# First layer's entry: output blocks 0 and 1 of the convolution's input product together, one half of the sequence at a time

## The chip, the cores and the metric

The kernel runs on one core of a Trainium2 chip. The metric is the device time of one execution in microseconds. The core's engines run side by side, each through a queue of its own in program order: TensorE (PE; its weight loads are listed as PEld), VectorE (DVE), ScalarE (ACT), GpSimd (POOL) and SyncE (SP, which here only issues loads from HBM). They wait for each other by semaphores.

## The reference, cut to what matters

A two-layer trunk on a sequence of 1024 rows with 1024 features, all in float32. The first layer starts with a conditioned norm, a product with a 1024x3072 matrix and a short gated convolution; the change is in that start alone. The rest (output product, MLP, a shared key/value side, attention, second MLP) follows unchanged.

```python
c_act = jax.nn.silu(c)
mod = c_act @ ada_w[l] + ada_b[l]                 # 1024 -> 6*1024; layer 0 here
sh_m, sc_m, g_m, sh_f, sc_f, g_f = jnp.split(mod, 6, axis=-1)
h = rmsnorm(x, norm_g[l, 0]) * (1 + sc_m) + sh_m  # modulate
bcx = h @ w_in                                    # 1024 x 3072
b_gate, c_gate, xh = jnp.split(bcx, 3, axis=-1)
u = c_gate * xh
conv = conv1d(u, w_conv, 3 taps, causal, per feature) + b_conv
y = (b_gate * conv) @ w_out
```

## The kernel before, in words

Every float32 product is made of three products of split operands: `hi` is the operand rounded to TensorE's reduced float32, `lo` what is left of it, and `mm` issues lo·hi, hi·lo, hi·hi into one accumulator. `split_w` makes the two parts, hi on ACT and lo on DVE.

The product `h @ w_in` has its output features in 8 blocks of 128 for each of the three parts g (b, c and x). Blocks 0 and 1 are computed directly in `conv_phase`; blocks 2 to 7 come after it in pairs with a scheme of seven products out of eight (`all_pairs`, `triple`), for which `conv_phase` leaves sums and differences of the halves of h (`sums`: t1 to t4). The first matmul of that pair phase needs the `uplo` part of its first weights, and its third group of twelve needs the split tile `s`.

h is made feature block by feature block (k = 0..7) and half by half (512 rows of the sequence each). Row tiles of x (`y` in the rows) are loaded, normed by `norm_x` (squares and root on ACT, scaling on DVE), turned by four transposes on TensorE (`turn`), then scaled and shifted while they leave PSUM: two ACT instructions (hi, and the full value) and one on DVE (lo), in `scaled`. Scale and shift of block k (`sh`) come from `ada(k)`, four loads of 256 KB (`aw`), a weighted sum over eight slices on DVE (eight instructions on `av`, the 8 values of silu(c) per partition as weights), two matmuls against a column of ones that add over the partitions, and two small DVE instructions (`ada_end`).

Before, the phase goes through k once for block m = 0, with half 0 ahead and half 1 two blocks of k behind (`LAG`), and then through k again for m = 1, both halves. The weights of w_in come in pieces of 128x384 (`w`): one per k and m. Four PSUM banks of `bank_ps` and two of `mm_ps` hold the accumulators of three g and two halves. `evict` reads them.

PE and SP stand in the written order in this phase (`pinned`). On DVE and ACT a scheduler sets the order when the program is built, also against the work behind the phase: the weighted sums of the next conditioning (`acc<-raw,csil,acc`) and the first splits of the pair phase (`uphi`, `uplo`, `s`) stand in DVE's and ACT's queues among the phase's own instructions.

Vectors (gains, biases, taps) are loaded as rows and turned by TensorE into columns, `vecs` and `bias`; the loads stand on ACT's queue.

Of the kernel before, what the change touches and what calls it, by code (L numbers as in the profile page):

```python
# [17 lines left out]
P = 128  # L18
# [30 lines left out]
def trunk_kernel(ctx: ExitStack, tc: tile.TileContext, x, c, ada_w, ada_b, norm_g, conv_in_w, conv_w,  # L49
# [5 lines left out]
    def nm(s):  # L55
        uid[0] += 1
        return f"{s}_{uid[0]}"
# [38 lines left out]
    def row_tile():  # L96
        return yp.tile([P, D], F32, tag="y", name=nm("y"), bufs=NT)
# [29 lines left out]
    vrows, brows = rows_[:, :P], rows_[:, P:2 * P]  # L127
    r = 0
    for src, n in ((norm_g.rearrange("l v (k p) -> (l v k) p", p=P), 64),
                   (conv_w[0].rearrange("w (k p) -> (w k) p", p=P), 24),  # L130
                   (conv_b.rearrange("o (k p) -> (o k) p", p=P), 8),
                   (kv_norm_g.rearrange("(k p) -> k p", p=P), 8),
                   (q_a_norm_g.rearrange("o (k p) -> (o k) p", p=P), 3),
                   (kv_a_norm_g.rearrange("(k p) -> k p", p=P), 2)):
        nc.scalar.dma_start(vrows[r:r + n, :], src)
        r += n
    nc.scalar.dma_start(brows[0:96, :], ada_b.rearrange("l (k p) -> (l k) p", p=P))
    nc.scalar.dma_start(brows[96:112, :], kv_ada_b.rearrange("(k p) -> k p", p=P))
# [722 lines left out]
    def conv_phase():  # L861
# [22 lines left out]
        nc.tensor.transpose(p_[:, :VEC_ROWS], vrows[:VEC_ROWS, :], ident[:VEC_ROWS, :VEC_ROWS])  # L884
        nc.vector.tensor_copy(vecs, p_[:, :VEC_ROWS])
        p_ = tp_ps()
        nc.tensor.transpose(p_[:, :BIAS_ROWS], brows[:BIAS_ROWS, :], ident[:BIAS_ROWS, :BIAS_ROWS])
        nc.vector.tensor_copy(bias, p_[:, :BIAS_ROWS])
        g1 = cp.tile([P, KD], F32, name="g1")
        b1 = cp.tile([P, KD], F32, name="b1")  # L890
        nc.vector.tensor_scalar(g1, gain(0, 0), RMS, None, op0=ALU.mult)
        nc.vector.scalar_tensor_tensor(b1, bias[:, 8:16], 1.0, g1, op0=ALU.add, op1=ALU.mult)
# [11 lines left out]
        def ada_end(k, raw):  # L904
            p_ = tp_ps()
            acc = st.tile([P, 2 * P], F32, tag="av", name=nm("av"), bufs=2)
            nc.vector.tensor_scalar(acc, raw[:, 0, :], csil[:, 0:1], None, op0=ALU.mult)
            for i in range(1, KD):
                nc.vector.scalar_tensor_tensor(acc, raw[:, i, :], csil[:, i:i + 1], acc, op0=ALU.mult, op1=ALU.add)  # L909
            for j in range(2):  # L910
# [22 lines left out]
        def weights(k, m):  # L933

            raw = ad.tile([P, D], F32, tag=("acc", "gmb")[k % 2], name=nm("w"), bufs=1)[:, :3 * P]
            ld(raw.rearrange("p (g m) -> p g m", g=3),
               conv_in_w[0][k * P:(k + 1) * P, :].rearrange("p (g c) -> p g c", g=3)[:, :, m * P:(m + 1) * P])
# [6 lines left out]
        def products(w, k, half, acc):  # L944
            for g in (1, 0, 2):
                mm(acc[g, half], [q[:, g * P:(g + 1) * P] for q in w], ops[("1", "2")[k // 4] + ("1", "2")[half]][k % 4],
                   k == 0, k == KD - 1)

        def evict(m, acc):
            b, c_, u, v = (row_tile() for _ in range(4))  # L950
            for half in range(2):
                sl = slice(half * HALF, (half + 1) * HALF)
                nc.scalar.activation(c_[:, sl], acc[1, half], AF.Copy)
                nc.scalar.activation(b[:, sl], acc[0, half], AF.Copy)
                nc.vector.tensor_tensor(u[:, sl], acc[2, half], c_[:, sl], op=ALU.mult)

            def end():
                conv(v, u, m, 0, S)
                nc.vector.tensor_tensor(v, v, b, op=ALU.mult)
                nc.scalar.dma_start(hd[m], v)  # L960

            late.append(end)

        def banks6():
            t_ = [bank_ps() for _ in range(4)] + [mm_ps(), mm_ps()]
            return {(g, half): t_.pop() for half in range(2) for g in (1, 0, 2)}

        def sums(kk):
            a, b = new[kk]
            c_, d = halves(row_tile())  # L970
# [15 lines left out]
        def first_half(k):  # L986
            raw = ada(k)
            if k == 0:
                load_x(0)
                norm_x(0)  # L990
            elif k == LAG:
                load_x(1)
            p_ = turn(k, 0)
            ada_end(k, raw)
            scaled(k, p_, old(k), ("11", "21")[k // 4])

        def second_half(k):
            if k < 4:
                new[k] = halves(raw_tile())
            scaled(k, turn(k, 1), new[k % 4][k // 4], ("12", "22")[k // 4])  # L1000

        with pinned([mybir.EngineType.PE, mybir.EngineType.SP]):
            w = [weights(0, 0)]
            first_half(0)
            acc = banks6()
            for k in range(KD + LAG):
                if k < KD - 1:
                    w.append(weights(k + 1, 0))
                    first_half(k + 1)
                if k < KD:  # L1010
                    products(w[k], k, 0, acc)
                if k == LAG:
                    norm_x(1)
                    second_half(0)
                if k >= LAG:
                    if k - LAG < KD - 1:
                        second_half(k - LAG + 1)
                    products(w[k - LAG], k - LAG, 1, acc)
                if k == KD:
                    w.append(weights(0, 1))  # L1020
            w = w[KD]
            st.release()
            evict(0, acc)
# [569 lines left out]
```

## Time and profile before

| | us |
|---|---|
| three runs, median (lowest, highest) | 2157.41 (2154.37, 2158.88) |
| profiled execution | 2159.2 |
| its span, first to last instruction | 2157.4 |
| PE busy in the span | 2062.0 (96%) |
| DVE busy, ACT busy | 1541.2 (71%), 1084.3 (50%) |
| first matmul of the pair phase starts at | 117.75 |

A matmul's busy time is modelled, so distances between starts say more than the busy time. An engine's idle time counts only where that engine carries the chain of work that ends last. The row of the granted clock has two levels for TensorE, 1.2 GHz (0.5) and 2.4 GHz (1.0).

### The profile page before, as it was taken

What the parts mean: (1) busy time and instruction counts of PE and PEld (TensorE: products, weight loads), DVE (VectorE), ACT (ScalarE), POOL (GpSimd) and SP (SyncE); (2) the same over time, 40 slices, a digit from 0 to 9 for tenths busy, and PEclk for the clock granted to TensorE, in tenths of its full rate; (3) what the DMA queues carried; (4) which work ended last, traced back from release to release, by engine and by line L of the source; (5) the groups of instructions that cost most, each with busy time, mean ns of one, the idle gap of its engine ahead of it and who ended that gap; (6) DMA issues with size and microseconds to landing.
All of it is one profiled execution on the core that took longest, in us unless ns stands there. A gap on an engine that the chain in (4) does not pass through costs nothing.

```text
span 2157.4 us, 25064 instructions
## 1 busy us (share of the span) xinstructions
PE 2062.0 (96%) x9438; PEld 1688.2 (78%) x9438; DVE 1541.2 (71%) x2087; ACT 1084.3 (50%) x1533; POOL 5.3 (0%) x13
## 2 busy tenths in 40 slices
PE   4999999989999999999899999999899999999998
PEld 3788878768888788888677788887678888788886
DVE  6877876876665669977688887756875665566576
ACT  4533353745554444455665565555744444544443
POOL 0000000000000000000000000000000000000000
PEclk9999999999999999999999999999999999999999
DMA  7444464254553889656223331143254653774355
GB/s 223 121 138 147 137 205 133 88 184 161 182 181 139 280 292 322 208 166 211 69 70 120 97 96 35 59 135 138 71 185 150 215 180 134 266 252 158 98 175 167
DMA packets 251023, 344.47 MB, mean 160 GB/s; under 512 B 19253, under 2 KB 142482, under 8 KB 250902
## 3 DMA queue, kind: packets, MB, share of 16 engines
q1 hardware_dynamic: 208408, 252.50, 37.4%
q10 hardware_dynamic: 42494, 90.38, 11.3%
q8 instruction: 74, 1.21, 0.2%
q14 instruction: 47, 0.39, 0.1%
HBM read 258.94 MB, written 83.89 MB: 159 GB/s over the span
## 4 chain that ended last, share of the span: by engine, by line
PE 77%; DVE 11%; ACT 6%; DMA 3%; issue 2%; ACTq 0%; SPq 0%; DVEq 0%
PE one L156 42%; PE mm L156 20%; PE tp L156 7%; PE big L156 3%; PE big L1360 2%; ACT junk L271 2%; DVE y L327 1%; PE tp L1386 1%; DVE raw L328 1%; DMA aw<-in_ada_w_dram 1%; ACT slot L1210 1%; DVE av L909 1%; PE tp L433 1%; DVE ring L160 1%; DVE acc L186 1%
## 5 line engine op out<-in xcount | busy, mean ns | idle before, releaser
L156 PE MATMUL one<-slot,uphi 128*128 128x512 f32 x1224 | 377.8, 389 | 0.0
L156 PEld LDWEIGHTS one<-slot,uphi 128*128 128x128 f32 x1224 | 230.4, 188 | 48.3 <-issue 0.5
L156 PE MATMUL one<-ring,ring 128*128 128x512 f32 x1152 | 262.9, 389 | 2.3 <-DVE ring L160 2.3
L160 DVE TENSOR_TENSOR uplo<-raw,uphi 128x1024 fp32r<-128x1024 f32 x127 | 153.3, 1222 | 143.1 <-ACT uphi L159 143.1
L156 PEld LDWEIGHTS one<-ring,ring 128*128 128x128 f32 x1152 | 215.9, 188 | 48.3 <-ACT ring L159 3.1
L156 PE MATMUL one<-slot,uplo 128*128 128x512 f32 x612 | 240.7, 393 | 8.2 <-DVE y L528 3.8
L160 DVE TENSOR_TENSOR ring<-raw,ring 128x1024 fp32r<-128x1024 f32 x144 | 174.3, 1220 | 55.6 <-ACT ring L159 55.3
L159 ACT ACTIVATE ring<-raw 128x1024 fp32r<-128x1024 f32 x144 | 149.5, 1052 | 106.6 <-DMA raw<-ha 61.6
L159 ACT ACTIVATE uphi<-raw 128x1024 fp32r<-128x1024 f32 x127 | 134.7, 1061 | 118.6 <-PE one L156 82.3
L156 PE MATMUL mm<-ring,ring 128*128 128x512 f32 x768 | 185.0, 390 | 1.6 <-DVE ring L160 1.6
L156 PE MATMUL tp<-ring,ring 128*128 128x512 f32 x768 | 183.9, 389 | 0.0
L159 ACT ACTIVATE ring<-w 128x1024 fp32r<-128x1024 f32 x80 | 84.8, 1060 | 178.7 <-PE tp L156 102.7
L156 PEld LDWEIGHTS mm<-ring,ring 128*128 128x128 f32 x768 | 143.7, 188 | 32.1 <-DVE ring L160 2.5
L156 PEld LDWEIGHTS tp<-ring,ring 128*128 128x128 f32 x768 | 144.1, 188 | 29.9
L160 DVE TENSOR_TENSOR ring<-w,ring 128x1024 fp32r<-128x1024 f32 x80 | 97.8, 1222 | 81.1 <-ACT ring L159 81.1
L156 PEld LDWEIGHTS one<-slot,uplo 128*128 128x128 f32 x612 | 115.2, 188 | 35.8 <-DVE y L528 5.5
L186 DVE SCALAR_TENSOR_TENSOR acc<-raw,csil,acc 128x1024 f32<-128x1024 f32 x88 | 112.5, 1278 | 22.8 <-DMA raw<-in_ada_w_dram 18.0
L526 ACT ACTIVATE y<-one 128x512 f32<-128x512 f32 x66 | 39.0, 591 | 159.6 <-PE one L156 118.5
L156 PE MATMUL mm<-slot,uphi 128*128 128x512 f32 x344 | 109.2, 399 | 9.6 <-DVE slot L398 9.4
L156 PE MATMUL one<-slot,s 128*128 128x512 f32 x468 | 112.9, 390 | 1.1 <-DVE s L160 1.1
L156 PEld LDWEIGHTS one<-slot,s 128*128 128x128 f32 x468 | 87.6, 188 | 20.6 <-DVE s L160 2.4
L156 PE MATMUL one<-q,uphi 128*128 128x512 f32 x328 | 101.9, 392 | 0.0
(267 smaller groups left out, 3614.4 us busy)
## 6 DMA issues: line engine op xcount, KB each, us to landing
ha<-y ACTq DMA_DIRECT2D x224, 256.0 KB, 4.0
raw<-ha SPq DMA_DIRECT2D x112, 512.0 KB, 4.0
raw<-in_ada_w_dram SPq DMA_DIRECT2D x80, 512.0 KB, 4.3
raw<-in_mlp_up_w_dram SPq DMA_DIRECT2D x70, 512.0 KB, 4.5
w<-in_mlp_down_w_dram SPq DMA_DIRECT2D x48, 512.0 KB, 7.0
raw<-in_mlp_down_w_dram SPq DMA_DIRECT2D x32, 512.0 KB, 4.0
raw<-in_conv_in_w_dram SPq DMA_DIRECT2D x18, 512.0 KB, 4.1
xs<-raw ACTq DMA_DIRECT2D x18, 512.0 KB, 2.8
```

Source lines behind the costliest of these rows:

```text
L156: nc.tensor.matmul(out_, lhs[a], rhs[b], start=first and i == 0, stop=last and i == 2, skip_group_check=more)
L159: nc.scalar.activation(hi, src, AF.Copy)
L160: nc.vector.tensor_tensor(lo, src, hi.bitcast(F32), op=ALU.subtract)
L186: nc.vector.scalar_tensor_tensor(acc, raw, s, acc, op0=ALU.mult, op1=ALU.add)
L271: nc.scalar.activation(junk, src, AF.Square, accum_out=ss)
L327: nc.vector.scalar_tensor_tensor(y, y, rroot(ss), self.gmb, op0=ALU.mult, op1=ALU.mult)
L328: nc.vector.tensor_tensor(xr, xr, y, op=ALU.add)
L433: nc.tensor.transpose(p_[:, t * P:(t + 1) * P], ys[half * 4 + t][:, k * P:(k + 1) * P], ident)
L526: nc.scalar.activation(dst, x_, AF.Copy)
L909: nc.vector.scalar_tensor_tensor(acc, raw[:, i, :], csil[:, i:i + 1], acc, op0=ALU.mult, op1=ALU.add)
L1210: nc.scalar.activation(y[32 * i:32 * i + 32, :], p_[32 * j:32 * j + 32, :], AF.Copy, scale=scale)
L1360: nc.tensor.matmul(o_, a, m_, start=j == 0, stop=j == 4)
```

## The change

Both output blocks m = 0 and 1 are computed together. A first pass over k does half 0 for both blocks, while scale and shift of block k arrive; a second pass does half 1 for both, from the weights' splits, all of which now stay (eight tiles each for hi and lo). A weight piece is 128x768 and holds both blocks: eight pieces instead of sixteen. Scale and shift of k = 0 and 1 are made by TensorE alone, sixteen matmuls of one column each with the loaded slices as weights, instead of the sum on DVE. x's first half is loaded first of all, its second half after all weights. Seven small row loads are cut into two groups: the gains of the norms and 96 rows of biases stay on ACT's queue, the others go to SP's, behind the loads of k = 0; the biases' transpose needs one of those. `sums` and the first stores take other buffers.

```diff
-    nc.scalar.dma_start(brows[96:112, :], kv_ada_b.rearrange("(k p) -> k p", p=P))
+    def later_rows():
+        ld(brows[96:112, :], kv_ada_b.rearrange("(k p) -> k p", p=P))
+        r = 0
...
+            ld(mrows[r:r + n, :], src)
+            r += n
...
-        def ada_end(k, raw):
-            p_ = tp_ps()
+        def ada_sum(raw):
             acc = st.tile([P, 2 * P], F32, tag="av", name=nm("av"), bufs=2)
...
+        def ada_end(k, raw, acc):
+            p_ = tp_ps()
             for j in range(2):
-                nc.tensor.matmul(p_[:, j:j + 1], acc[:, j * P:(j + 1) * P], ones[:, 0:1], start=True, stop=True)
+                cols = slice(j * P, (j + 1) * P)
+                if acc is not None:
+                    nc.tensor.matmul(p_[:, j:j + 1], acc[:, cols], ones[:, 0:1], start=True, stop=True)
+                else:
+                    for i in range(KD):
+                        nc.tensor.matmul(p_[:, j:j + 1], raw[:, i, cols], csil[:, i:i + 1], start=i == 0, stop=i == KD - 1)
...
-            w = [wr.tile([P, 3 * P], F32R, tag="w" + part_, name=nm("w"), bufs=4) for part_ in "hl"]
+            w = [wr.tile([P, 6 * P], F32R, tag="w" + part_, name=nm("w"), bufs=KD) for part_ in "hl"]
...
-        def products(w, k, half, acc):
+        def products(w, k, half, m, acc):
...
+            load_x(0)
+            raws, wraws, sums_, ws, turned = [], [], {}, [], {}
+
+            def fetch(k):
+                raws.append(ada(k))
+                wraws.append(weights(k))
+
+            fetch(0)
+            later_rows()
+            fetch(1)
+            feature_rows(vecs[:, :64], vrows[:64, :])
+            feature_rows(bias, brows[:BIAS_ROWS, :])
...
+            norm_x(0)
+
+            def scales(k):
+                ada_end(k, raws[k], sums_.get(k))
+                scaled(k, turned.pop(k), old(k), ("11", "21")[k // 4])
+                ws.append(weights_split(wraws[k]))
+
+            turned[0] = turn(0, 0)
+            scales(0)
+            turned[1] = turn(1, 0)
             acc = banks6()
-            for k in range(KD + LAG):
...
+            for k in range(KD):
+                if k + 2 < KD:
+                    fetch(k + 2)
+                    sums_[k + 2] = ada_sum(raws[k + 2])
+                elif k + 2 == KD:
+                    load_x(1)
+                    feature_rows(vecs[:, 64:VEC_ROWS], mrows[:VEC_ROWS - 64, :])
+                products(ws[k], k, 0, 0, acc)
+                if k + 1 < KD:
+                    scales(k + 1)
+                else:
+                    evict(0, 0, acc)
                     norm_x(1)
...
+                products(ws[k], k, 0, 1, acc)
+                if k + 2 < KD:
+                    turned[k + 2] = turn(k + 2, 0)
+            evict(1, 0, acc)
             st.release()
...
+            second_half(0, turn(0, 1))
+            second_half(1, turn(1, 1))
             acc = banks6()
             for k in range(KD):
-                w, w_ = weights(k + 1, 1) if k < KD - 1 else None, w
-                products(w_, k, 0, acc)
-                products(w_, k, 1, acc)
-                if k % 2 == 0:
-                    sums(k // 2)
-            evict(1, acc)
+                products(ws[k], k, 1, 0, acc)
+                if k + LAG < KD:
+                    second_half(k + LAG, turn(k + LAG, 1))
+                products(ws[k], k, 1, 1, acc)
+                if k + LAG >= 4 and k + LAG < KD:
+                    sums(k + LAG - 4)
+            for m in range(2):
+                evict(m, 1, acc)
```

PE's queue at the entry, before: the two transposes of the row vectors, then by k four transposes of x (`tp<-cs,y`) and the two matmuls against ones (`tp<-ones,av`), and the first products.

```order
L884 MATMUL tp_159<-cs,raw_82 128x109
L887 MATMUL tp_162<-cs,raw_82 128x112
L919 MATMUL tp_224<-cs,y_151 128x128
...
L911 MATMUL tp_229<-ones,av_230 128x1 x2
L919 MATMUL tp_263<-cs,y_151 128x128
...
L911 MATMUL tp_268<-ones,av_269 128x1 x2
L156 MATMUL mm_251<-slot_137,w_180 128x512
L156 MATMUL mm_251<-slot_137,w_179 128x512 x2
```

PE's queue at the entry, now (`tp<-csil,aw` is the conditioning by TensorE, sixteen matmuls for each of k = 0 and 1; w_255 is the lo part of the weights of k = 0, w_254 the hi part).

```order
L889 MATMUL tp_187<-cs,raw_82 128x64
L889 MATMUL tp_190<-cs,raw_82 128x112
L928 MATMUL tp_227<-cs,y_145 128x128
...
L920 MATMUL tp_232<-csil,aw_167 128x1 x16
L928 MATMUL tp_258<-cs,y_145 128x128
...
L158 MATMUL one_263<-slot_131,w_255 128x512
...
L920 MATMUL tp_294<-csil,aw_180 128x1 x16
L158 MATMUL one_266<-slot_131,w_255 128x512
```

The sixteen matmuls of k = 0 now stand between the first transposes and the first product, and those of k = 1 between the first product of block 0 and that of block 1.

DVE's queue in the first pass, now, from scale and shift of k = 1 on (w_317 is the lo part of the weights of k = 1, av_276 the weighted sum of k = 2, av_341 that of k = 3).

```order
L921 SCALAR_TENSOR_TENSOR sh_156<-tp_294,g_153,b_154 128x1
L923 TENSOR_TENSOR sh_156<-tp_294,bias 128x1
L935 TENSOR_TENSOR slot_131<-q_139,slot_131 128x512
L907 TENSOR_SCALAR av_276<-aw_269,csil 128x256
L162 TENSOR_TENSOR w_317<-w_185,w_316 128x768
L909 SCALAR_TENSOR_TENSOR av_276<-aw_269,csil,av_276 128x256 x5
L162 TENSOR_TENSOR w_368<-w_274,w_367 128x768
L909 SCALAR_TENSOR_TENSOR av_276<-aw_269,csil,av_276 128x256
L907 TENSOR_SCALAR av_341<-aw_334,csil 128x256
L909 SCALAR_TENSOR_TENSOR av_276<-aw_269,csil,av_276 128x256
```

The sum of k = 2 stands behind scale and shift of k = 1, so behind PE's sixteen matmuls for k = 1, and behind the split of the weights of k = 1.

DVE's queue at the end of the phase, before (uplo_1026, uplo_1059, s_201 and uplo_1069 are the pair phase's first splits; y_1007 is what the second block's last accumulators are read into).

```order
L160 TENSOR_TENSOR uplo_1026<-raw_1019,uphi_1025 128x1024
...
L160 TENSOR_TENSOR uplo_1059<-raw_1021,uphi_1058 128x1024
...
L160 TENSOR_TENSOR s_201_1064<-raw_1021,s_200_1063 128x512
L482 TENSOR_TENSOR raw_1019<-raw_1019,raw_1021 128x512
L186 SCALAR_TENSOR_TENSOR acc_1088<-raw_1096,csil,acc_1088 128x1024
L160 TENSOR_TENSOR uplo_1069<-raw_1019,uphi_1068 128x1024
L955 TENSOR_TENSOR y_1007<-one_756,y_1006 128x512
```

DVE's queue at the end of the phase, now (y_682 is read from the accumulator that PE finishes last, mm_715; uplo_987, uplo_1020 and s_172 are the same three splits).

```order
L970 TENSOR_TENSOR y_682<-mm_715,y_682 128x512
L188 SCALAR_TENSOR_TENSOR acc_1049<-raw_1052,csil,acc_1049 128x1024
L162 TENSOR_TENSOR uplo_987<-raw_980,uphi_986 128x1024
L188 SCALAR_TENSOR_TENSOR acc_1049<-raw_1054,csil,acc_1049 128x1024
L476 TENSOR_TENSOR raw_980<-raw_980,raw_982 128x512
L477 TENSOR_TENSOR raw_982<-raw_982 128x512
L188 SCALAR_TENSOR_TENSOR acc_1049<-raw_1057,csil,acc_1049 128x1024
L162 TENSOR_TENSOR uplo_1020<-raw_982,uphi_1019 128x1024
L481 TENSOR_TENSOR raw_982<-raw_982,raw_980 128x512
L484 TENSOR_TENSOR raw_980<-raw_980,raw_982 128x512
L162 TENSOR_TENSOR s_172_1025<-raw_982,s_171_1024 128x512
```

Before, the first splits stood ahead of the read of the last accumulator; now they stand behind it.

## Rows read from the trace of the kernel before

**Rows 1.** Windows: start:end, us, busy PE PEld DVE ACT POOL, clock, DMA share, GB/s.

```profile
0.00:117.53 117.53, 86.61 (x386) 69.47 (x386) 86.68 (x184) 60.76 (x103) 2.44 (x10) 0.97 0.62 179
117.53:200.00 82.47, 82.47 (x362) 67.60 (x361) 61.70 (x70) 27.81 (x35) 0.00 (x0) 1.00 0.40 124
```

**Rows 2.** Waits of PE, first 135 us: us in total, times, longest us.

```profile
PE tp L911 <- DVE av L909: 10.3, 4, 6.7
PE tp L884 <- DMA y<-in_x_dram: 9.6, 1, 9.6
...
PE tp L887 <- DMA raw<-in_kv_ada_b_dram: 2.7, 1, 2.7
```

**Rows 3.** Timeline of PE, end of the phase: start us, us, instruction, shapes, count.

```profile
115.03 2.88 PE L156 MATMUL one<-slot,w 128*128 128x512 f32 x12
117.75 0.39 PE L156 MATMUL one<-slot,uplo 128*128 128x512 f32 x1
123.19 1.07 PE L156 MATMUL one<-slot,s 128*128 128x512 f32 x4
```

**Rows 4.** Timeline of DVE, end of the phase; in brackets idle before and its releaser.

```profile
97.54 1.22 DVE L160 TENSOR_TENSOR uplo<-raw,uphi 128x1024 fp32r<-128x1024 f32 x1
...
110.21 0.68 DVE L160 TENSOR_TENSOR s<-raw,s 128x512 fp32r<-128x512 f32 x1
...
115.99 0.69 DVE L955 TENSOR_TENSOR y<-one,y 128x512 f32<-128x512 f32 x1 [2.13 <-PE one L156]
118.34 1.28 DVE L186 SCALAR_TENSOR_TENSOR acc<-raw,csil,acc 128x1024 f32<-128x1024 f32 x1 [1.67 <-DMA raw<-in_ada_w_dram]
```

**Rows 5.** Timeline of PE, 24 to 57 us.

```profile
24.46 0.98 PE L911 MATMUL tp<-ones,av 128*128 128x1 f32 x4 [1.89 <-DVE av L909]
25.31 2.91 PE L156 MATMUL mm<-slot,w 128*128 128x512 f32 x6
...
30.85 1.84 PE L156 MATMUL mm<-slot,w 128*128 128x512 f32 x6
...
55.68 0.60 PE L919 MATMUL tp<-cs,y 128*128 128x128 f32 x4
...
56.12 0.50 PE L911 MATMUL tp<-ones,av 128*128 128x1 f32 x4
56.48 1.63 PE L156 MATMUL mm<-slot,w 128*128 128x512 f32 x6
```

**Rows 6.** Windows of the loads and of the clock.

```profile
14.00:22.00 8.00, 3.09 (x11) 2.13 (x12) 6.61 (x18) 4.75 (x12) 0.00 (x0) 1.00 1.20 298
22.00:28.00 6.00, 4.11 (x13) 3.18 (x12) 5.12 (x14) 3.08 (x5) 0.00 (x0) 1.00 1.05 387
...
40.00:44.00 4.00, 3.50 (x10) 3.00 (x11) 3.12 (x9) 1.45 (x2) 0.00 (x0) 0.50 0.25 66
```

**Rows 7.** Timeline of ACT, norm of x's first and last tile of half 0.

```profile
10.55 1.06 ACT L271 ACTIVATE junk<-y 128x1024 bf16<-128x1024 f32 x1 [2.70 <-DMA y<-in_x_dram]
...
17.74 0.29 ACT L273 ACTIVATE small<-small,eps_d 128x1 f32<-128x1 f32 x1
```

**Rows 8.** Timeline of DVE, 41 to 45 us.

```profile
41.72 2.04 DVE L909 SCALAR_TENSOR_TENSOR av<-aw,csil,av 128x256 f32<-128x256 f32 x4
...
44.27 0.48 DVE L909 SCALAR_TENSOR_TENSOR av<-aw,csil,av 128x256 f32<-128x256 f32 x1
44.67 0.35 DVE L907 TENSOR_SCALAR av<-aw,csil 128x256 f32<-128x256 f32 x1
```

**Rows 9.** Groups by form, 0 to 117.5 us: count, busy us, mean ns, idle before.

```profile
L925 ACT ACTIVATE slot<-tp,sh 128x512 fp32r<-128x512 f32 x12 | 9.3, 778 | 21.7 <-DVE sh L914 19.0 <-DVE small L278 1.4 <-PE tp L919 1.3
...
L160 DVE TENSOR_TENSOR w<-w,w 128x384 fp32r<-128x384 f32 x16 | 8.8, 553 | 1.7 <-ACT w L159 1.7
...
L912 DVE SCALAR_TENSOR_TENSOR sh<-tp,g,b 128x1 f32<-128x1 f32 x8 | 1.7, 217 | 5.3 <-PE tp L911 5.3
```

**Rows 10.** Issues of loads, first 120 us: queue, count, KB, us to landing.

```profile
raw<-in_kv_ada_b_dram ACTq DMA_DIRECT2D x1, 8.0 KB, 5.6
```

More of the change, by code (lines that the diff above doesn't have):

```diff
@@ L126, in trunk_kernel @@
     rows_ = raw_tile()
[L127 to L136, printed above, removed]
[L137 to L138 removed]
+    vrows, brows, mrows = (rows_[:, i * P:(i + 1) * P] for i in range(3))
+    nc.scalar.dma_start(vrows[0:64, :], norm_g.rearrange("l v (k p) -> (l v k) p", p=P))
+    nc.scalar.dma_start(brows[0:96, :], ada_b.rearrange("l (k p) -> (l k) p", p=P))
+    def later_rows():
+        ld(brows[96:112, :], kv_ada_b.rearrange("(k p) -> k p", p=P))
+        r = 0
+        for src, n in ((conv_w[0].rearrange("w (k p) -> (w k) p", p=P), 24),
+                       (conv_b.rearrange("o (k p) -> (o k) p", p=P), 8),
+                       (kv_norm_g.rearrange("(k p) -> k p", p=P), 8),
+                       (q_a_norm_g.rearrange("o (k p) -> (o k) p", p=P), 3),
+                       (kv_a_norm_g.rearrange("(k p) -> k p", p=P), 2)):
+            ld(mrows[r:r + n, :], src)
+            r += n
     ones = cp.tile([P, P], F32, name="ones")
@@ L881, in load_x, with feature_rows @@
                 ld(xt[t], x0[t * P:(t + 1) * P, :])
-        p_ = tp_ps()
[L884 to L888, printed above, removed]
+        def feature_rows(dst, src):
+            p_ = tp_ps()
+            n = src.shape[0]
+            nc.tensor.transpose(p_[:, :n], src, ident[:n, :n])
+            nc.vector.tensor_copy(dst, p_[:, :n])
         g1 = cp.tile([P, KD], F32, name="g1")
         b1 = cp.tile([P, KD], F32, name="b1")
-        nc.vector.tensor_scalar(g1, gain(0, 0), RMS, None, op0=ALU.mult)
-        nc.vector.scalar_tensor_tensor(b1, bias[:, 8:16], 1.0, g1, op0=ALU.add, op1=ALU.mult)
         sh = [cp.tile([P, 2], F32, name=nm("sh")) for _ in range(KD)]
@@ L931, in conv_phase, with weights, weights_split @@
         new = [None] * 4
-        def weights(k, m):
-            raw = ad.tile([P, D], F32, tag=("acc", "gmb")[k % 2], name=nm("w"), bufs=1)[:, :3 * P]
+        def weights(k):
+            raw = ad.tile([P, D], F32, tag=("acc", "gmb")[k % 2], name=nm("w"), bufs=1)[:, :6 * P]
             ld(raw.rearrange("p (g m) -> p g m", g=3),
-               conv_in_w[0][k * P:(k + 1) * P, :].rearrange("p (g c) -> p g c", g=3)[:, :, m * P:(m + 1) * P])
-            w = [wr.tile([P, 3 * P], F32R, tag="w" + part_, name=nm("w"), bufs=4) for part_ in "hl"]
+               conv_in_w[0][k * P:(k + 1) * P, :].rearrange("p (g c) -> p g c", g=3)[:, :, :2 * P])
+            return raw
+        def weights_split(raw):
+            w = [wr.tile([P, 6 * P], F32R, tag="w" + part_, name=nm("w"), bufs=KD) for part_ in "hl"]
             split_w(w[0], w[1], raw)
@@ L942, in conv_phase, with evict @@
         late = []
-        def products(w, k, half, acc):
+        def products(w, k, half, m, acc):
             for g in (1, 0, 2):
-                mm(acc[g, half], [q[:, g * P:(g + 1) * P] for q in w], ops[("1", "2")[k // 4] + ("1", "2")[half]][k % 4],
+                mm(acc[m, g], [q[:, (2 * g + m) * P:(2 * g + m + 1) * P] for q in w], ops[("1", "2")[k // 4] + ("1", "2")[half]][k % 4],
                    k == 0, k == KD - 1)
[L949 to L955, printed above, removed]
+        kept_rows = [None, None]
+        def evict(m, half, acc):
+            if half == 0:
+                kept_rows[m] = [row_tile() for _ in range(2)]
+            b, u = kept_rows[m]
+            sl = slice(half * HALF, (half + 1) * HALF)
+            nc.scalar.activation(u[:, sl], acc[m, 1], AF.Copy)
+            nc.scalar.activation(b[:, sl], acc[m, 0], AF.Copy)
+            nc.vector.tensor_tensor(u[:, sl], acc[m, 2], u[:, sl], op=ALU.mult)
             def end():
+                v = row_tile()
                 conv(v, u, m, 0, S)
@@ L960, in end @@
                 nc.scalar.dma_start(hd[m], v)
-            late.append(end)
+            if half:
+                late.append(end)
         def banks6():
             t_ = [bank_ps() for _ in range(4)] + [mm_ps(), mm_ps()]
-            return {(g, half): t_.pop() for half in range(2) for g in (1, 0, 2)}
+            return {(m, g): t_.pop(0) for m in range(2) for g in (1, 0, 2)}
         def sums(kk):
             a, b = new[kk]
-            c_, d = halves(row_tile())
+            c_, d = halves(ad.tile([P, D], F32, tag=("acc", "gmb")[kk % 2], name=nm("w"), bufs=1))
             ops["t3"].append(block(kk))
@@ L984, in norm_x, with second_half @@
                 nc.vector.tensor_scalar(xt[t], xt[t], rroot(squares(nx, xt[t])), None, op0=ALU.mult)
[L986 to L997, printed above, removed]
+        def second_half(k, p_):
             if k < 4:
                 new[k] = halves(raw_tile())
-            scaled(k, turn(k, 1), new[k % 4][k // 4], ("12", "22")[k // 4])
+            scaled(k, p_, new[k % 4][k // 4], ("12", "22")[k // 4])
@@ L1021, in conv_phase @@
-            w = w[KD]
+            load_x(0)
[8 more added lines that the diff above has]
+            feature_rows(bias, brows[:BIAS_ROWS, :])
+            nc.vector.tensor_scalar(g1, gain(0, 0), RMS, None, op0=ALU.mult)
+            nc.vector.scalar_tensor_tensor(b1, bias[:, 8:16], 1.0, g1, op0=ALU.add, op1=ALU.mult)
```

19 lines of the change are left out of this document (2 added, 17 removed).

## Prediction

> **What bounds the kernel now.** I read the windows first, then PE's waits, then the timelines. The windows say where there is anything to win [rows 1]: in the entry phase PE is busy 86.6 of 117.5 us, behind it 82.5 of 82.5. From the pair phase on PE is the bound, without a gap, so the change is worth what it does to one moment: the start of the pair phase's first matmul, 117.75 us [rows 3]. The 30.9 us of PE's idle time in front of it are the whole stake. The waits split them [rows 2]: 9.6 us at the very start, until the first loads have landed, 2.7 more for the last bias row, and 10.3 us (one of 6.7) for DVE's weighted sums. The rest is pieces of one or two us. Then I looked at what stands ready when the phase ends [rows 4]: DVE made the first splits of the pair phase at 97.5 (`uplo`) and 110.2 (`s`), long before PE wants them at 117.75 and 123.19. The read of the last accumulators at 115.99 waits 2.13 us for PE and holds up nothing that PE needs.
>
> **The change, part by part.** PE's own work stays 288 matmuls of 512 columns and 64 transposes. At the upper rate twelve matmuls take 2.72 us (115.03 to 117.75) [rows 3], 0.227 each; four transposes 0.44 (55.68 to 56.12), the two matmuls of a conditioning block 0.36 (56.12 to 56.48) [rows 5]. At the lower rate the same are about 0.45 (2.91 for six, tail included) and 0.85 (24.46 to 25.31). The granted clock of 40 to 44 us is 0.50, which is 1.2 GHz [rows 6]; at PE's first start the rows say 1.00, but the spacing is that of the lower rate until about 31 us [rows 5, 6].
>
> *To the end of k = 0's conditioning (T0).* Before, the first x tile was normed from 10.55 on [rows 7], behind 0.2 MB of weights and 1.05 MB of slices; 1.77 MB at 298 GB/s [rows 6] are 5.9 us, so 4.6 us go to issue, first byte and completion. Now x comes first: at 387 GB/s, the rate of the stretch with x's other half [rows 6], its four tiles land at 6.0 to 10.0 us. From the first tile to the last root it took 7.5 us (10.55 to 18.03), with a weight split of 0.5 in it [rows 7]: 13.0, scaled at 13.9. The slices of k = 0 land at 13.5 (1.05 MB more at 298), the weights at 14.8, and behind those on the same queue the bias row that the biases' transpose waits for. PE takes its queue in order, so the transposes of x begin at about 15.3 and end at 16.2. Sixteen matmuls against two before: 8 x 0.85 = 6.8, T0 = 23.0.
>
> The bias row's landing, 5.6 us after its issue on ACT's queue [rows 10], was what PE waited for before, too [rows 2]. The Trainium skill (DMA: Bandwidth & Descriptors, "Queues, rings and completion order") says that each DMA engine takes turns between the queues that have work, packet by packet, so a small load on ACT's queue passes the large ones on SP's. The change takes that away. By that rule the row on its old queue would be there at about 12.7, as before, and T0 1.1 us earlier (x, at 13.9, then decides); by the queue order I use, 23.0. No run here shows the row on SP's queue.
>
> *To the end of k = 1's conditioning (T1).* Scale and shift, ACT's two instructions and DVE's lo: 0.4 + 1.5 [rows 9] + 0.7 (as the subtraction for `s`, [rows 4]), PE goes on at 25.65. Eight matmuls and the next sixteen: 1.8 + 2.9 at the upper rate, 3.6 + 6.8 at the lower, so T1 lies between 30.4 and 36.1. Sixteen one-column matmuls in a row don't occur before, so it is open whether they bring the clock up; before, the spacing fell 6.5 us after PE had begun to work through (24.46 to about 31) [rows 5]. I take T1 = 32: counted from T0, the same 6.5 us end at 29.5, when the eight matmuls (25.65 + 3.6) are through, and the sixteen run at the upper rate.
>
> *From T1 to k = 2.* DVE's queue decides, walked row by row as it now stands: scale and shift, ACT's scaling and the lo part end at T1 + 2.6. Then comes one step of the sum of k = 2, and then the split of the weights of k = 1, whose ACT half had to wait for the scaling of k = 1. A 768 wide split lies between 0.55 (384, [rows 9]) and 1.22 (1024, [rows 4]); I take 0.9. Five steps of the sum: 0.5 apart in a chain, 0.4 where another instruction stands between [rows 8]. With the split of k = 2's weights and the last steps the sum is ready at T1 + 8.1, PE has its scale and shift at T1 + 8.5. PE's work in that time is 4.5 us; it waits 4.
>
> *k = 3 to 7.* DVE per k: first step 0.3, seven steps 3.1 [rows 8], split 0.9, lo 0.6, scale and shift 0.2: 5.1. PE per k: 18 x 0.227 + 0.44 + 0.36 = 4.9. They are level, so each k costs the larger, plus what the lo part loses by standing among the sums, about 0.5: 5.6, five times 28. Then 2.05 (block 1 of k = 6), 0.5, and 3.9 for k = 7: half 0 ends at T1 + 43.1. Bounds: 4.9 per k if DVE never holds PE (3.5 us less), 6.6 if its interleaving costs a whole us more (5 us more).
>
> *Half 1.* Two groups of transposes, scaling, lo: PE waits 2.9 us at the change of halves, with x's second half long there. Sixteen groups of nine matmuls, 32.5, and six groups of transposes, 2.6: the phase ends at T1 + 81. DVE has 40 instructions of 0.6 to 0.7 there, 27 us, and keeps up. So the phase's matmuls end at 113, against 117.5: 4.5 us won.
>
> *The pair phase's start.* Here something is lost. The first splits now stand behind the read of the accumulator that PE finishes last. After PE's last matmul come that read (0.69), a step of a conditioning sum (1.28) and the split `uplo` (1.22) [rows 4]: 3.2 us in which PE has nothing. PE then has 24 matmuls, 5.4 us, to 8.6; `s` is ready only after another step (1.28), two sums of 0.6, a third step whose row must still land (about 6.4 + 1.2), a split of 1.15 (the same spacing as its 1.22 busy, less the overlap), two more of 0.6 and ACT's and DVE's parts of `s`: 10.8. Another 2.15. Together 5.35, between 0 and 8.
>
> The Trainium skill (TensorE: Matmul & The Clock Gate, "Architectural detail") says that VectorE's queue is strictly first in, first out, and that only TensorE pulls anything forward. By it the whole 5.35 is paid; if DVE could begin `uplo` while the read waits, nothing. The trace has no counterexample: behind the read at 115.99 nothing started during its wait of 2.13 [rows 4].
>
> *Sum.* 113.1 + 5.35 = 118.5 for the first gapless stretch, against 117.6: 0.9 us longer. The rest of the kernel is unchanged and PE-bound. The profiled execution took 2159.2, so 2160; the median of the runs shown is 1.8 below it, so 2158.3 there. I have counted no wait that I can't name, and add 0.7: 2159.
>
> **Rivals.** *Lower rate until T1 (slower).* Place: the two times sixteen matmuls. For it: at the start of before, the spacing fell only with full-width matmuls under way [rows 5]. Against it: PE is occupied without a gap from 16 us on. Price: T1 = 36, 4 us more, in all 5 more than before: 2163. It decides if the first products still have the 0.45 spacing at 29 us. Chance 0.18.
>
> *Loads late (slower).* The slices of k = 4 stand on SP's queue behind the weights of k = 3, and these wait for the split of k = 1 at T1 + 3.7. 1.44 MB at 298 GB/s and 3 us of latency put them at T1 + 11.5, and DVE wants the first half at T1 + 12.1. If each load comes 2 us later than that, DVE waits about 1.4 us in each of five k: 7 us, 2165. For it: PE's longest wait, 6.7 us for a sum [rows 2], came in the stretch with the densest loads. Against it: the second and later k have 2 us and more in hand. It decides from a wait of DVE for `aw` of over 1 us a k. Chance 0.15.
>
> *PE bound from k = 2 on (faster).* T1 = 30.4 and 4.9 per k: 1.6 + 3.5 less, 4.2 below before: 2153.5; without the wait at the pair phase 2148. For it: sums of two k are interleaved, which saves the chain's 0.1 per step. Against it: DVE's 5.1 is an even match at best. Chance 0.17.
>
> *Forecast:* no change that can be told, 0.5. About 0.2%, 4.3 us, is what a measurement of this kernel can tell from no change.
>
> **How the numbers follow.** The forecast's own range is T1 from 30.4 to 34 and the lower end of the waits, 2155 to 2162. To hold 8 in 10 it goes up over both slower rivals, to 2167, and down to half of the faster one with part of the pair phase's wait gone, 2149. Slower by over 0.2%: the two slower rivals nearly whole, less what of them stays within, 0.3. Faster: the faster rival and a little of the forecast's lower side, 0.2. Within: 0.5.
>
> **What would show it.** T0 near 23 and T1 near 32 in PE's timeline; the first pair matmul near 118 behind a gap of 3 us, and a second gap of 2 us before `s`; PE's wait for DVE `uplo` and `s` in its list of waits. If no such gaps are there, the term of 5.35 is wrong and the result is faster; if DVE waits for `aw`, the loads rival holds; if the spacing of the first products is 0.45, the clock rival.

## The result, and the profile after

The changed kernel takes 2167.02 us (median of 4 runs, 2163.4 to 2168.67) against 2156.96 for the one before (4 runs): ratio 1.0037, 95% interval 1.002 to 1.0054. The medians lie 10 us apart (0.47%), by the ratio of the runs it is slower by 0.37%, where 2159 and no change that can be told were forecast. The profiled execution took 2163.4 us, the lowest of the four; its span is 2161.5, 4.1 above that of before.

The windows of the changed kernel, cut where PE's last matmul of the phase ends, in the columns of [rows 1]:

```profile
0.00:116.15 116.15, 95.77 (x443) 78.10 (x443) 68.43 (x149) 55.89 (x91) 2.44 (x10) 0.97 0.52 151
116.15:200.00 83.85, 79.38 (x339) 64.45 (x339) 69.53 (x79) 29.16 (x36) 0.00 (x0) 0.98 0.51 156
```

Against [rows 1], PE idles 20 us in the phase where it idled 31, but its busy time rose by 9, and the stretch behind, gapless before, now has 4.5 us of idle time. DVE's work in the phase fell by 18 us (86.7 to 68.4). From PE's waits, first 135 us:

```profile
PE tp L917 <- DVE av L909: 0.9, 1, 0.9
```

The waits for DVE's sums [rows 2] fell from 10.3 to 0.9 us, as the change has it; a wait of 3.97 us for `uplo`, which before lay ready 19 us early [rows 4], is new. PE's timeline, to be read against [rows 3, 5]:

```profile
14.85 0.42 PE L889 MATMUL tp<-cs,raw 112*128 112x112 f32 x1 [10.74 <-DMA raw<-in_kv_ada_b_dram]
...
16.63 6.99 PE L920 MATMUL tp<-csil,aw 128*128 128x1 f32 x32 [0.51 <-DVE bias L890]
...
26.26 3.40 PE L158 MATMUL one<-slot,w 128*128 128x512 f32 x8 [0.60 <-DVE slot L935]
29.50 4.07 PE L920 MATMUL tp<-csil,aw 128*128 128x1 f32 x32
...
41.84 0.58 PE L917 MATMUL tp<-ones,av 128*128 128x1 f32 x4 [0.85 <-DVE av L909]
...
77.72 1.03 PE L928 MATMUL tp<-cs,y 128*128 128x128 f32 x8
...
114.63 1.52 PE L158 MATMUL mm<-slot,w 128*128 128x512 f32 x6
120.12 0.50 PE L158 MATMUL one<-slot,uplo 128*128 128x512 f32 x1 [3.97 <-DVE uplo L162]
...
128.00 3.06 PE L158 MATMUL one<-slot,s 128*128 128x512 f32 x12 [0.50 <-DVE s L162]
```

The sixteen one-column matmuls of a block show as 32 instructions. T0 is 16.63 + 6.99 = 23.6, T1 is 33.57, the phase ends at 116.15, and `s` is used at 128.00 against 123.19 [rows 3]: 4.8 us later. Matching PE's matmuls one by one against before, the distance is 4.2 to 5.0 nearly everywhere from there to the end (2.5 and 5.9 at the extremes), so the span's 4.1 us are the entry's.

### The profile page after: what moved, and what is told of

It is laid out like the page before. It is cut to its first block, busy times and chain, and to the rows that moved or that the text cites. A ratio compares the mean times of both kernels' runs of the same rounds, so it can differ in the third digit from the quotient of the medians.

```text
span 2161.5 us, 25112 instructions
## 1 busy us (share of the span) xinstructions
PE 2073.2 (96%) x9495; PEld 1698.2 (79%) x9495; DVE 1534.0 (71%) x2064; ACT 1082.2 (50%) x1525; POOL 5.3 (0%) x13
## 4 chain that ended last, share of the span: by engine, by line
PE 78%; DVE 12%; ACT 7%; DMA 2%; issue 2%; ACTq 0%; SPq 0%; DVEq 0%
PE one L158 42%; PE mm L158 20%; PE tp L158 7%; PE big L158 3%; PE big L1392 2%; ACT junk L273 2%; DVE y L329 1%; PE tp L1418 1%; DVE raw L330 1%; ACT slot L1242 1%; DVE acc L188 1%; DMA raw<-hd 1%; PE tp L435 1%; DVE ring L162 1%; PE tp L920 1%
```

## The experiments

Each was timed in five rounds against the kernel before, on one chip per group. T1 (end of block 1's conditioning on PE) and the start of the first `s` matmul are read from each profile's timeline of PE.

| kernel | conditioned by TensorE | T1 | `s` at | median us | ratio, 95% interval |
|---|---|---|---|---|---|
| before | none | 25.4 | 123.2 | 2157.2 to 2157.7 | |
| change, again | 0, 1 | 36.6 | 131.2 | 2167.53 | 1.0044, 1.0032 to 1.0056 |
| new order, sums on DVE | none | 26.0 | 118.4 | 2153.36 | 0.9982, 0.9974 to 0.9991 |
| new order, block 1 only | 1 | 30.7 | 124.1 | 2159.44 | 1.0007, 0.9998 to 1.0016 |
| old order | 0, 1 | 35.0 | 132.3 | 2171.41 | 1.0064, 1.0051 to 1.0078 |

The theory after the result: the one-column matmuls, at TensorE's lower rate, put more on the path than the sums they replace. The rivals: the order, and the new wait at the pair phase's start.

**The change again** (no edit).

> The changed kernel itself once more, for its size beside the others. Its profiled execution ended 4.1 us above the one of before, the median of its four runs 10.1 us. If the entry phase is all of the loss, the first pair-phase matmul and the total move together, and a profile with a total near 2167 shows a later end of the phase (a later rise of PE's rate, T1 2 to 5 us later) or a longer stretch at the lower rate behind the gap at the pair phase's start. If the loss is elsewhere, the phase ends near 116 again and the difference of 4 to 6 us appears behind 200 us. Ratio to before between 1.002 and 1.0054.

2167.53 us in 6 runs. The profiled execution took 2170.72, and its timeline of PE differs from the first one's where it counts:

```profile
26.25 3.78 PE L158 MATMUL one<-slot,w 128*128 128x512 f32 x8 [0.60 <-DVE slot L935]
29.82 6.82 PE L920 MATMUL tp<-csil,aw 128*128 128x1 f32 x32
...
123.21 0.50 PE L158 MATMUL one<-slot,uplo 128*128 128x512 f32 x1 [3.97 <-DVE uplo L162]
...
126.14 0.63 PE L158 MATMUL one<-slot,uplo 128*128 128x512 f32 x1
126.57 1.05 PE L158 MATMUL one<-slot,uphi 128*128 128x512 f32 x2
...
131.20 3.03 PE L158 MATMUL one<-slot,s 128*128 128x512 f32 x12 [0.66 <-DVE s L162]
```

Block 1's 32 instructions take 6.82 us, as block 0's do, not 4.07: T1 is 36.6, 3.1 later, and `s` 3.2 later. So the first profile had caught an execution in which the higher rate came early. What its span has beyond that comes at the very end, where nothing was changed: from the entry to 2100 us this execution stands 6 to 9 us behind before, and 4 more from 2128 us of before on. There PE waits 1.98 us for one of DVE's splits (0.65 before), and the thirty matmuls behind the next wait run in part at the lower rate. Before, then the repeat:

```profile
2130.61 7.11 PE L156 MATMUL mm<-ring,ring 128*128 128x512 f32 x30 [0.98 <-DVE ring L160]
```
```profile
2139.62 9.72 PE L158 MATMUL mm<-ring,ring 128*128 128x512 f32 x30 [0.90 <-DVE ring L162]
```

From 2140 to 2145 us of the repeat the granted clock is 0.50, at the same place before 1.00: 1.3 and 2.6 us make up the 4. No such end stands in the first profile, so these are of the execution and not of the change.

**Only the order: both sums back on DVE.**

```diff
+            for k in range(2):
+                sums_[k] = ada_sum(raws[k])
             turned[0] = turn(0, 0)
             scales(0)
```

> Undoes one part: scale and shift of blocks 0 and 1 by DVE's sums again, everything else as changed. Theory A (the sixteen matmuls stand on the path, nearly all at the lower rate, while DVE sits idle from 17 to 34 us): T0 falls from 23.6 to 17 to 19, T1 from 33.6 to 24 to 26, the phase ends 7 to 9 us earlier, total 7 to 9 us below the changed kernel. Rival B (the loads are the bound of the first pass, so an earlier T1 is given back by waits for slices): T1 is earlier, DVE waits for slices by 1 us or more per block, and the total moves by less than 3 us.

2153.36 us in 11 runs: 14 below the change, nearly twice what was expected, and 0.18% faster than before, its interval clear of 1. PE and, below, DVE:

```profile
16.65 1.01 PE L917 MATMUL tp<-ones,av 128*128 128x1 f32 x4 [0.75 <-DVE av L909]
...
25.05 0.98 PE L917 MATMUL tp<-ones,av 128*128 128x1 f32 x4 [0.96 <-DVE av L909]
...
118.37 3.04 PE L158 MATMUL one<-slot,s 128*128 128x512 f32 x12 [0.42 <-DVE s L162]
```
```profile
12.01 0.35 DVE L907 TENSOR_SCALAR av<-aw,csil 128x256 f32<-128x256 f32 x1
...
13.98 2.04 DVE L909 SCALAR_TENSOR_TENSOR av<-aw,csil,av 128x256 f32<-128x256 f32 x4
```

DVE makes block 0's sum from 12.0 on, while PE still waits for the bias row, so block 0 is conditioned at 17.7 instead of 23.6, block 1 at 26.0 instead of 36.6. The sums were not in the way here; DVE had the time. `s` comes 12.8 us earlier than in the repeat of the change.

**Block 0 on DVE, block 1 by TensorE** (`sums_[0]` alone).

> The change with block 0's sum on VectorE and block 1's alone by TensorE. Measured: both on VectorE 2153.4, both by TensorE 2167.5, 14.1 between them. Theory A, each block costs its own 32 small matmuls on the path at the lower rate: block 0 is ready at 17.7 as with both on VectorE, the products follow at 20.3, the 32 small ones take 6.8 from 24, so block 1's conditioning ends near 31 instead of 25.6: 2158.7 (2157 to 2161). Theory B, most of the cost is block 0's, which holds up the first product while all else waits, and block 1's is hidden behind VectorE's sum of block 2: 2155 or less. Theory C, the cost comes from both together through TensorE's rate: below 2157 or above 2162.

2159.44 us, at theory A's 2158.7. PE's timeline:

```profile
23.82 6.83 PE L920 MATMUL tp<-csil,aw 128*128 128x1 f32 x32
```

T1 is 30.7 (31 was expected). Block 1 by TensorE costs 6.1 us, block 0 the other 8.1, around the 6.8 us of a block's one-column matmuls; T1 moves by 4.6 and 6.0, the start of `s` by 5.7 and 7.1. So neither block's share is hidden behind other work.

**The other part alone: TensorE conditions blocks 0 and 1 in the old order.**

```diff
         def ada_end(k, raw):
             p_ = tp_ps()
...
+            if k > 1:
...
             for j in range(2):
...
+                cols = slice(j * P, (j + 1) * P)
+                if k > 1:
+                    nc.tensor.matmul(p_[:, j:j + 1], acc[:, cols], ones[:, 0:1], start=True, stop=True)
+                else:
+                    for i in range(KD):
+                        nc.tensor.matmul(p_[:, j:j + 1], raw[:, i, cols], csil[:, i:i + 1], start=i == 0, stop=i == KD - 1)
```

> The kernel before, in its own order, with one part of the change: the conditioning of blocks 0 and 1 by TensorE, 16 matmuls a block, in place of VectorE's sums. Its block 1's conditioning ends at 25.4 today. Theory A, the old order has room for it: block 1's conditioning ends about 5 to 6 later, but TensorE's wait of 6.67 us for VectorE's sum of block 3 shrinks by as much, since VectorE has 16 operations less to do: 2155 to 2159, no measurable difference. Theory B, the small matmuls are paid in full as in the new order: 6 to 14 slower, 2163 to 2171.

2171.41 us, 14.0 above before; I had expected theory A. The wait of 6.67 us that should have shrunk [rows 2] is still there, 9.7 us later. PE, then DVE:

```profile
19.22 6.83 PE L917 MATMUL tp<-csil,aw 128*128 128x1 f32 x32
...
27.96 6.99 PE L917 MATMUL tp<-csil,aw 128*128 128x1 f32 x32 [0.42 <-ACT q L931]
...
50.19 0.99 PE L914 MATMUL tp<-ones,av 128*128 128x1 f32 x4 [6.88 <-DVE av L910]
```
```profile
26.75 0.35 DVE L908 TENSOR_SCALAR av<-aw,csil 128x256 f32<-128x256 f32 x1
27.95 0.69 DVE L932 TENSOR_TENSOR slot<-q,slot 128x512 fp32r<-128x512 f32 x1 [0.85 <-ACT q L931]
34.99 0.22 DVE L918 SCALAR_TENSOR_TENSOR sh<-tp,g,b 128x1 f32<-128x1 f32 x1 [6.35 <-PE tp L917]
...
35.19 2.04 DVE L910 SCALAR_TENSOR_TENSOR av<-aw,csil,av 128x256 f32<-128x256 f32 x4
```

DVE has begun the sum of block 2 at 26.75 and then stands 6.35 us in front of block 1's scale, which PE delivers; the sum's other steps are queued behind it. So the work taken off DVE became a wait of DVE. With this the two parts add up: the order -3.8, TensorE's conditioning +14.0, together +10.2; the change measures +10.1 to +10.4. This profile is only some 9 us behind before all along. The other 5 us are a matter of which executions were profiled: this one, 2168.33, lies 3.1 below the median of its runs, and before's, 2159.2, lies 1.8 above that of its own.

**TensorE kept busy before its start.** To see what the lower rate is worth, 18 matmuls of the identity ahead of the bias rows' transpose (their result is not used).

```diff
+            p_ = tp_ps()
+            for i in range(18):
+                nc.tensor.matmul(p_[:, :P], ident, ident, start=True, stop=True)
             feature_rows(bias, brows[:BIAS_ROWS, :])
```

> The change, with 18 matmuls of the identity by itself (128 columns, result unused) on TensorE ahead of the bias rows' transpose, in the stretch from 4 to 14.6 us where TensorE has nothing to do. Measured so far: in the repeated profile of the change the 64 small matmul instructions of blocks 0 and 1 take 6.99 and 6.82 us, and the first products stand at twice the later spacing; block 1's conditioning ends at 36.5. Theory A, the lower rate is what makes the small matmuls dear: the 64 take about 3.4 us a block, the first products 1.7 less, block 1's conditioning ends at 27 to 29, and the time falls by about 8 to 2159.5 (2157 to 2162). Theory B, a small matmul costs the same at either rate: only the nine products and the later ones gain, 2 to 3 us, about 2165. Theory C, the rate falls again during the small matmuls, as it did at 32.6 us in the first profile of the change: a gain of 3 to 5, about 2163.

2164.53 us, 1.0032 (1.002 to 1.0043), 3 below the change:

```profile
6.25 5.91 PE L1022 MATMUL tp<-cs 128*128 128x128 f32 x36
15.50 0.29 PE L889 MATMUL tp<-cs,raw 112*128 112x112 f32 x1 [3.34 <-DMA raw<-in_kv_ada_b_dram]
...
17.27 6.99 PE L920 MATMUL tp<-csil,aw 128*128 128x1 f32 x32 [1.01 <-DVE bias L890]
...
30.34 3.86 PE L920 MATMUL tp<-csil,aw 128*128 128x1 f32 x32
```

The added matmuls end at 12.2, and 3.3 us of idle time follow. Block 0's one-column matmuls run at the lower rate again (granted clock 0.50 from 17 to 30 us); only block 1's do not, and T1 is 2.4 earlier. That is theory C's size for another reason: the rate had fallen before them. At the higher rate the 32 instructions take 3.86 us, the last two of them at the lower rate again, so a one-column matmul does get cheaper with the rate, which rules theory B out, but two blocks would still cost some 7 us.

The same 18 matmuls in the version with both parts of the next paragraph:

> The same 18 matmuls in the kernel with both blocks' sums on VectorE and the first splits early (2152.8 measured). Theory A: there block 1's conditioning waits for VectorE's sum (0.96 us in the trace), so a faster TensorE gains at most that wait's rest: 0 to 1 us, about 2152.3. Theory B, TensorE's products bound that stretch as well: the nine products of block 0 take 2.1 instead of 3.8, a gain of 1.7 or more, 2151 or less.

2155.0 us (0.9984, 0.9975 to 0.9993), no gain; PE there waits for DVE's sums as before, and in the profiled execution the higher rate came later: the three matmuls behind block 1's conditioning take 1.63 us at 26.20, and 0.94 at 25.50 without the 18.

**The pair phase's start.** The first weights' splits were put ahead of the last reads (a part of the weights' pool released first, `load_pair`, `up_split` and `pair_sums` of the first pair written before `evict`), once in the change, once with the sums on DVE.

```diff
...
+            wr1.release()
+            up = pool("up", "right")
+            ready = [load_pair(conv_in_w[0], 5)]
+            ready.append(up_split(up, ready[0][0]))
+            ready.append(list(pair_sums(up, *ready[0])))
             for m in range(2):
                 evict(m, 1, acc)
...
```

> The changed kernel with the pair phase's first weights loaded, split and summed ahead of the last reads of the accumulators (the weights' tiles of k = 0 to 4 give their room back earlier for it). Theory A (the gap of 4.0 us before the first uplo, and the lower rate for 4 us behind it, are a loss that DVE's order makes): PE has no gap before uplo and stays at 2.4 GHz, a gap of about 1.5 us is left before s: 4 to 5 us below the changed kernel. Rival B (DVE is too full at the end of the phase, so that the splits only move the wait to the reads or to s): less than 2 us.

> Both edits together: sums of blocks 0 and 1 on DVE, first splits of the pair phase early. Theory A: the two gains add, 11 to 13 us below the changed kernel, so 1 to 3 us below before. Rival B (one hides the other: with an earlier phase the loads for the pair phase come too late): the sum is at least 3 us short of the two single gains.

2166.25 us (1.0041, 1.0029 to 1.0053) and 2152.79 (0.998, 0.9971 to 0.9989): 1.3 and 0.6 us below the versions without it, neither measurable and far less than the wait of 3.97. PE's timeline of the first:

```profile
118.91 0.39 PE L158 MATMUL one<-slot,uplo 128*128 128x512 f32 x1
...
127.56 5.49 PE L158 MATMUL one<-slot,s 128*128 128x512 f32 x12 [3.05 <-DVE s L162]
```

The wait for `uplo` is gone and 3.05 us of waiting for `s` stand in its place, with the rate's loss behind it: twelve matmuls 5.49 instead of 2.88. DVE, full with `sums` to the phase's end, is late with one or the other. I then put off the three background steps of the first pair (`run_bg(0 if len(late) == 2 else 3)`), one of which stands in DVE's queue ahead of each split:

> The change itself with the three background steps of the first pair job put off to the second, and nothing else. In its trace one such accumulation (1.27 us) stands ahead of the split that ends TensorE's wait of 3.97 us for uplo, two more ahead of the one that ends the wait for s, and the matmuls between stand at twice the later spacing for 3 us. Theory A, VectorE's queue at the pair phase's start is the second term of the loss: uplo comes 1.2 earlier, s 2 to 4 earlier, 2163.5 to 2165.5. Theory B, the loss all lies in the entry: no change, 2167.3.

> Both blocks' sums on VectorE and the first splits early (2152.8 measured), with the three background steps (the accumulations of the next scale vector, 1.28 us each on VectorE) of the first pair job put off to the second. In that kernel's trace TensorE waits 3.05 us for s at 114 with one such accumulation ahead of it on VectorE, and the 12 matmuls behind the wait take 5.49 instead of 2.88. Theory A, VectorE's queue at that place is the bound: the wait falls by 1.2, and if the 12 matmuls keep the higher rate the gain is up to 3.8: 2149 to 2151.6. Theory B, s waits for the products of the first splits anyway, or what is put off comes back behind it: 2152.8.

In the change 2167.01 us (1.0046, 1.0032 to 1.006), with both other parts 2153.47 (0.9983, 0.9974 to 0.9992): nothing in either. PE's timeline of the first:

```profile
122.06 0.50 PE L158 MATMUL one<-slot,uplo 128*128 128x512 f32 x1 [2.79 <-DVE uplo L162]
...
129.23 2.88 PE L158 MATMUL one<-slot,s 128*128 128x512 f32 x12
```

In the change `uplo` comes 1.15 and `s` 1.97 earlier than in its repeat, as theory A says, but at 404 us of before this kernel stands 7.4 us behind, the repeat 6.9: what was gained is given back in the pairs that follow. Every edit at this place moved a wait and not the end.

**The bias row back on ACT's queue.**

```diff
+    nc.scalar.dma_start(brows[96:112, :], kv_ada_b.rearrange("(k p) -> k p", p=P))
     def later_rows():
-        ld(brows[96:112, :], kv_ada_b.rearrange("(k p) -> k p", p=P))
```

> The change with the one row of kv_ada_b loaded by ScalarE's queue right behind ada_b's, as before, instead of by SyncE's behind block 0's conditioning weights. In the change that row ends TensorE's wait at 14.85 us, and the small matmuls of block 0 start at 16.63. Theory A, the row's place in the queue holds block 0 up: x is normalized at 13.6, so its transposes and the small matmuls start 1.2 to 1.8 earlier, and the time falls by as much, to about 2166 (2165 to 2167). Theory B, the transfers of block 0's weights (the 1 MB that lands at the same time) end the wait as well, so it changes nothing: 2167.5.

2167.26 us (1.0039, 1.0025 to 1.0053): no change in time, though T0 moved. PE, then ACT:

```profile
7.98 0.42 PE L889 MATMUL tp<-cs,raw 112*128 112x112 f32 x1 [1.68 <-DMA raw<-in_kv_ada_b_dram]
...
13.77 6.83 PE L920 MATMUL tp<-csil,aw 128*128 128x1 f32 x32
...
24.24 4.21 PE L158 MATMUL one<-slot,w 128*128 128x512 f32 x9 [2.15 <-DVE w L162]
28.24 6.82 PE L920 MATMUL tp<-csil,aw 128*128 128x1 f32 x32
```
```profile
21.02 0.78 ACT L934 ACTIVATE slot<-tp,sh 128x512 fp32r<-128x512 f32 x1 [8.55 <-DVE sh L923]
...
22.36 0.84 ACT L161 ACTIVATE w<-w 128x768 fp32r<-128x768 f32 x1
```

The row lands 6.9 us earlier and T0 is 20.6, 3.0 earlier. But when the program is built, the split of block 0's weights is now placed behind the scaling of block 0 on ACT, which waits 8.55 us for the scale; PE waits for that split, and T1 is 35.1, only 1.6 earlier, less than the runs can tell.

## Why the prediction failed where it did, step by step

| step | forecast | first profile | repeat |
|---|---|---|---|
| T0 | 23.0 | 23.6 | 23.6 |
| T1 | 32 | 33.6 | 36.6 |
| k = 2 conditioned, after T1 | 8.5 | 8.85 | 8.85 |
| half 0 ends, after T1 | 43.1 | 44.2 | 44.2 |
| matmuls of the phase end, after T1 | 81 | 82.6 | 82.6 |
| lost from there to `s` | 5.35 | 6.4 | 6.5 |

(Lost to `s`: its start less the phase's end and 5.44 for the 24 matmuls at the upper rate: 128.00 - 116.15 - 5.44.)

**The step that failed is T1.** "I take T1 = 32 ... and the sixteen run at the upper rate": in the repeat they ran at the lower one, 6.82 us, and 4.6 us of the miss are there. The bounds given, 30.4 to 36.1, miss it by 0.5 because T0 came 0.6 late, and the rival *Lower rate until T1* is what happened: block 1's 32 instructions took 6.8 to 7.0 us in the repeat, with the early splits, with the background later, with the row on ACT's queue, in the old order and alone, and about 4 only in the first profile and behind the added matmuls; its test, first products at a spacing of 0.45 at 29 us, is met (eight in 3.78 us from 26.25). Its price was 2163. That the stated range reaches up to the measured time is owed to the loads rival, which did not occur. The clock was argued from 6.5 us of PE's work before [rows 5], a single place, and against the rival stood that PE is occupied without a gap from 16 us on. PE was occupied, in the repeat from 16.6 to 42.6 us with no wait over 0.6, and yet the spacing fell only then. And where the higher rate did come early it did not last: in the first profile it was there from 29.1 to 32.5 us and then again only from 39.3.

**The pair phase's start was there but too small.** Both gaps were forecast (3.2 and 2.15 us), and came as 3.97 and 0.5 to 0.66, with 1.9 us between them that no step had: after the gap PE's matmuls stand at twice the spacing (126.14 to 126.57, 0.43, where the higher rate gives 0.23). The profile's windows show it; the first is the repeat's idle stretch, the last follows 2 us after PE's return:

```profile
121.00:123.00 2.00, 0.00 (x0) 0.00 (x0) 2.00 (x2) 0.00 (x0) 0.00 (x0) 1.00 0.99 367
...
125.00:126.00 1.00, 1.00 (x4) 0.80 (x3) 0.68 (x1) 0.24 (x1) 0.00 (x0) 0.50 0.50 139
```

And a fourth DVE instruction stood in the queue, a subtraction of `sums` (L997) in front of the last read. DVE of the repeat:

```profile
119.55 0.68 DVE L997 TENSOR_TENSOR q<-w,q 128x512 fp32r<-128x512 f32 x1
120.15 0.68 DVE L970 TENSOR_TENSOR y<-mm,y 128x512 f32<-128x512 f32 x1
120.75 1.27 DVE L188 SCALAR_TENSOR_TENSOR acc<-raw,csil,acc 128x1024 f32<-128x1024 f32 x1
121.94 1.22 DVE L162 TENSOR_TENSOR uplo<-raw,uphi 128x1024 fp32r<-128x1024 f32 x1
```

The rule cited for it (the Trainium skill, TensorE: Matmul & The Clock Gate, "Architectural detail": VectorE's queue is strictly first in, first out) agrees with these rows and with DVE's 6.35 us of standing still in the old order. It should have been put to the other place too: by it a scale that PE delivers late holds up every sum behind it.

**What was right.** T0, within 0.6, and that the bias row decides it; the walk through DVE's queue for k = 2 and the 5.5 to 6.0 us per k (5.6 forecast); half 1. The load rival did not occur: no wait for `aw` is among DVE's waits of the phase. Nor did the faster one.

The rule on queues (the Trainium skill, DMA: Bandwidth & Descriptors, "Queues, rings and completion order": each DMA engine takes turns between the queues that have work, so a small load on another queue passes large ones) agrees with the run: on ACT's queue the row ended PE's wait at 7.98, on SP's at 14.85. The 1.1 us that the prediction gave it were 3.0 at T0, and nothing at the end.

**The question not asked.** The prediction priced TensorE's conditioning at 6.8 us a block and compared the sum with before as a whole; it never set the two parts against each other. The rows had it: a sum on DVE takes 4 us ([rows 8]: eight steps of about 0.5), DVE was about to be relieved in that stretch anyway, and TensorE's way was 6.8. What the relieved engine did is in the repeat's rows of DVE, 17.4 us of waiting for PE:

```profile
23.64 0.22 DVE L921 SCALAR_TENSOR_TENSOR sh<-tp,g,b 128x1 f32<-128x1 f32 x1 [6.88 <-PE tp L920]
...
36.68 0.22 DVE L921 SCALAR_TENSOR_TENSOR sh<-tp,g,b 128x1 f32<-128x1 f32 x1 [10.49 <-PE tp L920]
```

The sum came out level because a gain of 4 and a loss of 14 stood in one line, the loss mis-sized.

Two things stay open: what decides whether the higher rate comes at 29 or at 43 us, and some 2 of the 10 us between the medians: `s` is 8.0 us late in the repeat, and what else its profile shows comes at the very end of that one execution.

## What to carry to other kernels

Split a change into its parts before pricing it: here one part gained 4 us, the other lost 14, and leaving the second out beats the kernel before (2153.4, and 2152.8 with the first splits early, which is no measurable difference). Work taken off an idle engine and put on the one that carries the path is a loss even where each piece is short; look at what the relieved engine then does, which here was to wait for the result. When an early matmul is to be priced, take the lower rate unless the trace shows the higher one at that very place.

## What the runs showed of the hardware

- One column is not cheap: at the lower rate a float32 matmul of 128x128 by one column takes 0.43 us (16 in 6.82), as long as one of 512 columns in reduced float32 there (eight in 3.78); at the higher rate 0.22 (two instructions 0.112 apart), where one of 512 columns takes 0.227.
- The same program, at the same place, ran these at the lower rate in one execution and for the most part at the higher in another, while the granted clock reads 1.00 in both windows below. The trace's first entry for the clock stands where the spacing falls, at 42.6 us in the repeat and at 29.1 in the first profile, and before its first entry the column reads 1.00 for want of one. So there the spacing tells the rate and the column doesn't. The repeat, then the first profile, in which the rate fell again while PE worked without a wait:

```profile
30.00:33.00 3.00, 3.00 (x17) 3.00 (x15) 0.00 (x0) 0.00 (x0) 0.00 (x0) 1.00 0.00 0
```
```profile
30.00:32.00 2.00, 2.00 (x20) 2.00 (x20) 0.00 (x0) 0.00 (x0) 0.00 (x0) 1.00 0.00 0
...
34.00:36.00 2.00, 2.00 (x6) 1.61 (x5) 0.54 (x1) 2.00 (x3) 0.00 (x0) 0.50 0.00 0
```

- The higher rate came, to stay until the pair phase, at 39.3 to 47.2 us in the six profiles of the new order with both blocks conditioned by TensorE, at 35.3 with block 1 alone, and at 24.5 to 32.3 in the four with the sums on DVE. Whether the one-column matmuls hold the rate down or only put off the work behind them, no run here separates.
- A wait of PE costs more than its length: 3.97 us without work were followed by 1.9 us of loss at 1.2 GHz, 3.05 us by at least 2.6, and 1.98 and 0.90 us close together at the repeat's end by 2.6.
- Matmuls without a purpose, ended 3.3 us before the real work, did not keep the rate up for it.
